# Places of an adding weight load, and of the sums and casts that wait for such loads, in a two-layer fp32 network kernel

## The chip, the cores and the metric

The kernel runs on one core of a Trainium2 chip. The metric is device time in microseconds of one execution; three executions of the kernel before gave 1048.98, 1050.86 and 1052.87, with a median of 1050.86.

The engines' names in the profile: PE multiplies matrices, DVE (VectorE) and ACT (ScalarE) work element by element, POOL (GpSimd) here issues mostly loads that add to what stands in the target, SP (SyncE) issues plain loads. Each engine works through its own list of instructions in order. A load is issued by an engine and then carried out by 16 DMA engines that all loads share.

## What is computed

The network has two residual layers over 512 tokens of 1024 features. Layer 0 mixes tokens by chunked attention, layer 1 by a gated linear recurrence. After each mixer comes the part that this case is about, a feed-forward block with a hidden size of 4096:

```python
D_MODEL = 1024; SEQ = 512; D_FF = 4 * D_MODEL

def rmsnorm(x, g):
    return x * lax.rsqrt(jnp.mean(x * x, axis=-1, keepdims=True) + RMS_EPS) * g

def sq_relu_mlp(h, w1, w2):
    z = jax.nn.relu(jnp.einsum('bsd,df->bsf', h, w1))
    return jnp.einsum('bsf,fd->bsd', z * z, w2)

for layer in range(2):
    h = h + mix[layer](rmsnorm(h, norm_mix[layer]))
    h = h + sq_relu_mlp(rmsnorm(h, norm_mlp[layer]), mlp_w1[layer], mlp_w2[layer])
return rmsnorm(h, norm_final)
```

All is float32.

## The kernel before

**Three matmuls for a product.** A float32 operand is split into a high part, rounded to the type that PE multiplies in one pass, and the rest, the low part. A product is made of high times high, high times low and low times high (`mm3`, L278 to L280). For weights, ACT makes the high part by a cast (`wh`, L178) and DVE the low part by a subtraction (`wl`, L181), piece by piece: a piece is 128 x 1024 numbers, 512 KB. There are five buffers each for `wh` and `wl`. The rows of the order below number the pieces: `wh47` and `wl47` are made from the 47th piece of the kernel.

**Fewer products by sums of blocks.** The feed-forward block multiplies 2 x 2 blocks in Strassen's manner, with seven products in place of eight, and some of the right operands are sums of weight blocks. For each group of the first weight matrix (`group(p, g)`, L806) the seven pieces are, in order: `u11`; `us1`, the sum of the blocks 21 and 22; `us2`, which is u11 + us1; `u12`; `us3`, which is u11 + 21; `us4`, u12 + us2; and `u22`. The second weight matrix gives seven pieces of two halves each: 11; t1, which is 12 + 11; 22; 21; t2; t3; t4. The plan (`add_mlp`, L237) mixes the two kinds in the order in which PE takes them.

Where the sums are made:
- `us1` needs no arithmetic engine: SP loads block 21 into the tile `kept` (L134), and POOL then issues a load of block 22 that adds to it (L136). The other half of `kept` takes block 22 alone.
- `us2` is a sum on DVE (L161). Behind it POOL issues the load of block 21 that adds to u11 in place, which makes `us3` (L163); it has to wait until `us2` and the `wl` of u11 have read u11.
- t1 is made by adding the loaded 11 to the loaded 12 by POOL's loads (`first_sum`, L123), t4 by one of L174. `us4`, t2 and t3 are sums on DVE.

**What sets the order.** The function `fetch` (L138) writes out, for the next piece, its sums, its cast and its subtraction, and then the loads that follow once its buffers are free. `want(1)` takes a piece and fetches on until three more are ready. The order in which an engine finally gets its instructions is made by the framework's scheduler from the order of the program and its own estimates; an instruction under `tc.keep_in_program_order` stays behind the instruction that the program writes just ahead of it on that engine.

**The first loads of a feed-forward block.** `first()` (L781) runs four pieces of the block's start (`up`), and there the attention or recurrence layer's residual tiles come free; one of them becomes `kept` for the groups from 1 on. Then come the loads of 11 and 12 of the second matrix (`load_down`, L118), the adding loads of `first_sum`, and group 0's second half (`group(0, 1)`) with, between its pieces, `opening`, the load of `kept` for group 1, the loads of 22 and 21, and `lengths`, eight sums of squares on ACT (`dsq`, L966) with the norm's reciprocal roots on DVE (`rq`, L776 to L779).

On PE, `m` are products of the first matrix (256 columns, 24 matmuls a piece), `x` and `y` of the second (512 columns). `a` is what the first matrix's products become by relu and square (L824, L825 on ACT, L820 a sum of two products on DVE). `hs`, `h` and `ls`, `l` are high and low parts of sums of `a`.

Of the kernel before, what the change touches and what calls it, by code (L numbers as in the profile page):

```python
# [35 lines left out]
def f(ap):  # L36
    return ap.bitcast(F32)
# [3 lines left out]
def trunk(ctx: ExitStack, tc: tile.TileContext, xT, cols, gfin, win, wqkv, wo, rwin, rga, rgx, rwo, w1, w2, out):  # L41
    nc = tc.nc
    V, S, G, PE = nc.vector, nc.scalar, nc.gpsimd, nc.tensor
# [57 lines left out]
    raws, start_, down, upper = {}, [], {}, {}  # L101

    def two(t):
        return t.rearrange("p (k c) -> p k c", k=2)

    def four(t):
        return t.rearrange("p (k c) -> p k c", k=4)

    def rows(src):
        return src.rearrange("(k p) c -> p k c", p=P)  # L110

    def load_down(key, name):
        if key not in down:
            return
        both = state["raw"].tile([P, 2, 1024], F32, name=f"b{name}_{key[0]}{key[1]}", tag=f"b{name}")
        for h in range(2):
            raws[name, h] = both[:, h]
            nc.sync.dma_start(two(raws[name, h]), rows(down[key][name][h * U : (h + 1) * U]))  # L118

    def first_sum(key):  # L120
        if key in down:
            for h in range(2):
                G.dma_start(raws["12", h], raws["11", h], accum_op=ALU.add)  # L123

    def load_up(key, name):
        if key not in upper:
            return
        if name in ("s1", "22"):
            raw = state["kept"][:, int(name == "22")]
        else:  # L130
            n = state["base"] + int(name == "12")
            raw = wraw.tile([P, 1024], F32, name=f"u{name}_{key[0]}{key[1]}", tag=f"wr{n % 3}")
        raws["u" + name] = raw
        nc.sync.dma_start(four(raw), rows(upper[key]["21" if name == "s1" else name]))  # L134
        if name == "s1":
            G.dma_start(four(raw), rows(upper[key]["22"]), accum_op=ALU.add)  # L136

    def fetch():  # L138
        i = state["next"]
        state["next"] += 1  # L140
        kind, nk, key = plan[i]
        H = wsp.tile([P, 1024], F32R, name=f"wh{i}", tag="wh")
        L = wsp.tile([P, 1024], F32R, name=f"wl{i}", tag="wl")
        n, half = 1024, nk
        if kind[:5] == "plain":
            n = nk * sum(src.shape[1] for src in key)
            raw = wraw.tile([P, 1024], F32, name=f"wr{i}", tag=f"wr{state['plain'] % 3}")
            state["plain"] += 1
            rv = raw[:, :n].rearrange("p (k c) -> p k c", k=nk)
            c0 = 0  # L150
            for n_, src in enumerate(key):
                w = src.shape[1]
                queue = nc.scalar if i == 0 and n_ else nc.sync
                queue.dma_start(rv[:, :, c0 : c0 + w], rows(src))
                c0 += w
        elif kind[0] == "u":
            nk = 4
            following = (key[0], key[1] + 1)
            if kind == "us2":
                raws["us2"] = wraw.tile([P, 1024], F32, name=f"us2_{key[0]}{key[1]}", tag=f"wr{(state['base'] + 2) % 3}")  # L160
                V.tensor_add(raws["us2"], raws["u11"], raws["us1"])  # L161
                raws["us3"] = raws["u11"]
                G.dma_start(four(raws["us3"]), rows(upper[key]["21"]), accum_op=ALU.add)  # L163
            if kind == "us4":
                raws["us4"] = raws["u12"]
                V.tensor_add(raws["us4"], raws["us4"], raws["us2"])
            raw = raws[kind]
        else:
            nk = 2
            following = (key[0], key[1] + 1)  # L170
            raw = raws[{"t1": "12", "t2": "22", "t3": "11", "t4": "21"}.get(kind, kind), half]
            if kind == "t2":
                V.tensor_add(raw, raw, raws["12", half])
                G.dma_start(raws["21", half], raw, accum_op=ALU.add)  # L174
            if kind == "t3":
                V.tensor_sub(raw, raws["22", half], raw)
        if i:
            S.copy(H[:, :n], raw[:, :n])  # L178
        else:
            start_.append(V.tensor_copy(H[:, :n], raw[:, :n]))  # L180
        low = V.tensor_sub(L[:, :n], raw[:, :n], f(H[:, :n]))  # L181
        if not i:
            start_.append(low)
        if kind == "plain_":
            state["base"] = state["plain"] % 3
            load_up((nk_layer[i], 0), "11")
            load_up((nk_layer[i], 0), "12")
        elif kind == "us2" and key[1]:
            load_up(following, "s1")
        elif kind == "us3":  # L190
            load_up(following, "11")
        elif kind == "us4":
            load_up(following, "12")
        elif kind == "u22" and key[1]:
            load_up(following, "22")
        elif kind == "t2" and half:
            load_down(following, "12")
        elif kind == "t3" and half:
            load_down(following, "11")
        elif kind == "t4" and half:  # L200
            first_sum(following)
            load_down(following, "22")
            load_down(following, "21")
        state["ready"].append((nk, H[:, :n].rearrange("p (k c) -> p k c", k=nk), L[:, :n].rearrange("p (k c) -> p k c", k=nk)))
# [466 lines left out]
    def mlp(ly, norm):  # L671
        with ExitStack() as mctx:
# [8 lines left out]
            low_, high = hB[0], hB[1]  # L681
# [68 lines left out]
            def up(p, j):  # L750
                WH, WL = want(1)
                acc = mmp(f"u{ly}{p}{j}")
                project([acc], [slice(0, P)], WH, WL, xs)
                for h in range(2):
                    if j % 4 == 0:
                        a[p, j // 4, h] = take(F32, f"a{p}{j // 4}{h}")
                    c = a[p, j // 4, h][:, j % 4]
                    S.activation(c, acc[:, h * U : (h + 1) * U], AF.Relu)
                    S.activation(c, c, AF.Square)
                if j == 0:  # L760
                    turn()
                if j == 1:
                    for k in range(KT):
                        scaled(k)
                if j == 2:
                    for n in (1, 3, 2, 4):
                        right(n)
                if j == 3:
                    for n in (1, 3, 2, 4):
                        right_split(n)  # L770
# [10 lines left out]
            def first():  # L781
                state["kept"] = sr.tile([P, 2, 1024], F32, name=f"kept0{ly}", tag="b21")
                load_up((ly, 0), "s1")
                load_up((ly, 0), "22")
                for j in range(4):
                    up(0, j)
                state["kept"] = per.tile([P, 2, 1024], F32, name=f"kept{ly}", tag="hx1")
                load_down((ly, 0), "11")
                load_down((ly, 0), "12")
                first_sum((ly, 0))  # L790
                here = group(0, 1)
                next(here)
                opening(0)
                load_up((ly, 1), "s1")
                next(here)
                load_down((ly, 0), "22")
                for n in range(4):
                    next(here)
                load_down((ly, 0), "21")
                load_up((ly, 1), "22")  # L800
                next(here)
                sums(0, False)
                sums(0, True)
                lengths()
# [56 lines left out]
            low, raw, turn_ = {}, {}, [0]  # L861
# [10 lines left out]
            def opening(p):  # L872
                raw["11"], raw["s1"], raw["s3"] = a[p, 0, 0], a[p, 0, 1], take(F32, f"s3{p}")
                ins = V.tensor_sub(raw["s3"], raw["11"], raw["s1"])
                if (ly, p) == (0, 1):
                    constants(ins)
                split("11", p)

            def sums(p, last):
                if last:  # L880
                    raw["s4"] = take(F32, f"s4{p}")
                    V.scalar_tensor_tensor(raw["s4"], raw["12"], -1.0, raw["s2"], ALU.mult, ALU.subtract)
                else:
                    raw["12"], raw["22"], raw["s2"] = a[p, 1, 0], a[p, 1, 1], take(F32, f"s2{p}")
                    V.tensor_sub(raw["s1"], raw["22"], raw["s1"])
                    V.scalar_tensor_tensor(raw["s2"], raw["22"], -1.0, raw["s3"], ALU.mult, ALU.subtract)
                    split("s1", p)
# [385 lines left out]
```

## Time and profile before

| | us |
|---|---|
| median of three executions | 1050.86 |
| the profiled execution | 1050.44 |
| its span, first to last instruction | 1048.7 |
| PE busy | 1023.1 |
| DVE busy | 876.6 |
| ACT busy | 667.2 |
| POOL busy | 91.0 |

The granted clock of PE was 0.992 of full speed on average. A row of a timeline has start, duration, engine, line of the kernel, operation, written and read tiles (without their numbers), and in brackets how long the engine had idled before and what released it. An engine may stand for long without loss where the work that it does later is not yet wanted; PE is the engine whose idle time counts as long as it is the busiest.

The times of loads are from issue to landing. With 0.5 MB each, a plain load of `kept` or `u` took 5.1 us in the median, an adding load of `kept` 6.0 and of `u` 6.3.

### The profile page before, as it was taken

Reading aid. Unit: us, or ns where it says so; the run is one execution under the profiler, and the core shown is the slowest. Engines: PE = TensorE matmul, PEld = TensorE weight load, DVE = VectorE, ACT = ScalarE, POOL = GpSimd, SP = SyncE. Lnnn points to the kernel's source line nnn. Section 1 sums busy time; section 2 is a strip of 40 time slices with the busy share of each in tenths; the row PEclk is TensorE's granted clock in tenths of the full one; section 3 lists DMA queues with packets and bytes.
Section 4 is the critical chain, followed back from the end, with each engine's and each line's share of the span. In section 5 each row is a group of like instructions: output and inputs, shape, how many; then the busy total and the mean of one; then the engine's idle time right before and its main releaser. Section 6 shows DMA issues by size and latency. Waiting matters only on the chain.

```text
span 1048.7 us, 15295 instructions
## 1 busy us (share of the span) xinstructions
PE 1023.1 (98%) x5762; PEld 894.3 (85%) x5762; DVE 876.6 (84%) x1230; ACT 667.2 (64%) x1020; POOL 91.0 (9%) x120
## 2 busy tenths in 40 slices
PE   9999999999899999999999999999899999999996
PEld 7788888888889999999987788888889999999985
DVE  7898779869489889789699989988389789789697
ACT  7667557647476567567567686656477567567565
POOL 1000000003101111111000000003101101101000
PEclk9999999999989999999999999999999999999999
DMA  8444354255948748737614412185848738737413
GB/s 270 114 129 132 82 165 116 61 148 134 240 101 219 177 87 220 202 61 202 181 21 114 128 61 81 58 231 124 230 101 221 201 61 221 202 61 201 122 41 100
DMA packets 122730, 147.34 MB, mean 140 GB/s; under 512 B 6304, under 2 KB 94368, under 8 KB 122656
## 3 DMA queue, kind: packets, MB, share of 16 engines
q1 hardware_dynamic: 101664, 112.09, 34.4%
q0 software_dynamic: 20416, 33.56, 18.5%
q8 instruction: 45, 0.74, 0.3%
q10 hardware_dynamic: 576, 0.72, 0.2%
q14 instruction: 29, 0.24, 0.1%
HBM read 119.07 MB, written 2.10 MB: 116 GB/s over the span
## 4 chain that ended last, share of the span: by engine, by line
PE 81%; DVE 9%; DMA 5%; issue 2%; SPq 1%; ACT 1%; POOL 0%; DVEq 0%; ACTq 0%; POOLq 0%
PE m L278 8%; PE m L280 8%; PE m L279 8%; PE x L279 5%; PE x L280 5%; PE x L278 5%; PE y L278 4%; PE y L279 3%; PE y L280 3%; DMA kept<-in_w 3%; DVE wl L181 3%; PE x L504 2%; PE wo L278 1%; PE wo L279 1%; PE v L278 1%
## 5 line engine op out<-in xcount | busy, mean ns | idle before, releaser
L178 ACT CAST wh<-b 128x1024 fp32r<-128x1024 f32 x112 | 117.0, 1052 | 85.6 <-PE m L279 44.2
L181 DVE TENSOR_TENSOR wl<-b,wh 128x1024 fp32r<-128x1024 f32 x112 | 136.1, 1222 | 39.2 <-ACT wh L178 38.5
L278 PE MATMUL m<-rH,wh 128*128 128x256 f32 x448 | 127.4, 284 | 12.7 <-DVE a L820 12.7
L280 PE MATMUL m<-rH,wl 128*128 128x256 f32 x448 | 127.1, 284 | 0.0
L279 PE MATMUL m<-rL,wh 128*128 128x256 f32 x448 | 127.0, 284 | 0.0
L278 PEld LDWEIGHTS m<-rH,wh 128*128 128x128 f32 x448 | 86.3, 193 | 14.3 <-DVE a L820 13.1
L178 ACT CAST wh<-wr 128x1024 fp32r<-128x1024 f32 (+1 forms) x65 | 66.7, 1029 | 44.6 <-PE wo L279 11.7
L280 PE MATMUL m<-hnH,wl 128*128 128x256 f32 x336 | 95.0, 283 | 0.0
L279 PE MATMUL m<-hnL,wh 128*128 128x256 f32 x336 | 95.0, 283 | 0.0
L278 PE MATMUL m<-hnH,wh 128*128 128x256 f32 x336 | 94.9, 282 | 0.0
L279 PEld LDWEIGHTS m<-rL,wh 128*128 128x128 f32 x448 | 86.4, 193 | 1.2
L280 PEld LDWEIGHTS m<-rH,wl 128*128 128x128 f32 x448 | 86.3, 193 | 0.0
L181 DVE TENSOR_TENSOR wl<-wr,wh 128x1024 fp32r<-128x1024 f32 (+1 forms) x66 | 78.1, 1187 | 7.7 <-ACT wh L178 7.4
L178 ACT CAST wh<-u 128x1024 fp32r<-128x1024 f32 x56 | 58.8, 1050 | 39.0 <-PE x L280 13.5
L181 DVE TENSOR_TENSOR wl<-u,wh 128x1024 fp32r<-128x1024 f32 x56 | 68.3, 1220 | 9.6 <-ACT wh L178 9.6
L279 PEld LDWEIGHTS m<-hnL,wh 128*128 128x128 f32 x336 | 64.3, 191 | 0.8
L278 PEld LDWEIGHTS m<-hnH,wh 128*128 128x128 f32 x336 | 64.2, 191 | 0.8
L280 PEld LDWEIGHTS m<-hnH,wl 128*128 128x128 f32 x336 | 64.3, 191 | 0.0
L278 PE MATMUL x<-wh,h 128*128 128x512 f32 (+1 forms) x132 | 50.8, 385 | 1.7 <-DVE d L1047 1.7
L279 PE MATMUL x<-wl,h 128*128 128x512 f32 (+1 forms) x132 | 50.9, 386 | 0.0
L280 PE MATMUL x<-wh,l 128*128 128x512 f32 (+1 forms) x132 | 50.9, 385 | 0.0
L278 PE MATMUL y<-wh,hs 128*128 128x512 f32 x128 | 50.2, 392 | 0.0
(382 smaller groups left out, 2894.9 us busy)
## 6 DMA issues: line engine op xcount, KB each, us to landing
b<-in_w SPq DMA_DIRECT2D x64, 512.0 KB, 5.9
b<-b POOLq DMA_DIRECT2D x32, 512.0 KB, 7.6
kept<-in_w SPq DMA_DIRECT2D x28, 512.0 KB, 5.1
u<-in_w SPq DMA_DIRECT2D x28, 512.0 KB, 5.1
wr<-in_wqkv SPq DMA_DIRECT2D x20, 512.0 KB, 4.1
wr<-in_rwin SPq DMA_DIRECT2D x16, 512.0 KB, 3.6
kept<-in_w POOLq DMA_DIRECT2D x14, 512.0 KB, 6.0
u<-in_w POOLq DMA_DIRECT2D x14, 512.0 KB, 6.3
```

The lines of the kernel that those rows point to most:

```text
L178: S.copy(H[:, :n], raw[:, :n])
L181: low = V.tensor_sub(L[:, :n], raw[:, :n], f(H[:, :n]))
L278: PE.matmul(acc, WH, XH, start=start, stop=False, skip_group_check=more)
L279: PE.matmul(acc, WH, XL, start=False, stop=False, skip_group_check=more)
L280: PE.matmul(acc, WL, XH, start=False, stop=stop, skip_group_check=more)
L504: PE.transpose(b[:, c : c + P], pt[:, seg[t] + kt * P : seg[t] + (kt + 1) * P], ident)
```

## The change

Three edits.

1. The sum `us2` on DVE stays behind what the program writes ahead of it on DVE.
2. So does the cast on ACT for the four kinds that have an adding load behind them: us1, us3, t1 and t4.
3. In `first()`, the plain load and the adding load of `kept` for group 1 are written ahead of the loads of 11 and 12, where they stood behind `opening`.

```diff
@@ fetch
             if kind == "us2":
                 raws["us2"] = wraw.tile([P, 1024], F32, name=f"us2_{key[0]}{key[1]}", tag=f"wr{(state['base'] + 2) % 3}")
-                V.tensor_add(raws["us2"], raws["u11"], raws["us1"])
+                tc.keep_in_program_order(V.tensor_add(raws["us2"], raws["u11"], raws["us1"]))
                 raws["us3"] = raws["u11"]
                 G.dma_start(four(raws["us3"]), rows(upper[key]["21"]), accum_op=ALU.add)
...
         if i:
-            S.copy(H[:, :n], raw[:, :n])
+            high = S.copy(H[:, :n], raw[:, :n])
+            if kind in ("us1", "us3", "t1", "t4"):
+                tc.keep_in_program_order(high)
@@ first
                 state["kept"] = per.tile([P, 2, 1024], F32, name=f"kept{ly}", tag="hx1")
+                load_up((ly, 1), "s1")
                 load_down((ly, 0), "11")
                 load_down((ly, 0), "12")
                 first_sum((ly, 0))
                 here = group(0, 1)
                 next(here)
                 opening(0)
-                load_up((ly, 1), "s1")
                 next(here)
```

Behind the second edit all lines stand two further down: L820 of before is L822 of the changed kernel.

What the edits move was read off the instructions of both programs, engine by engine. The rows have the line, the operation, and written and read tiles with their piece or block and a buffer number. First SP's queue in layer 0's feed-forward block, from the first load of block 12 of the second matrix. Before:

```order
L118 DMA b12_00_2765<-in_w2 128x2x512 x2
L134 DMA kept0_2761<-in_w1 128x4x256
L118 DMA b22_00_2843<-in_w2 128x2x512
L134 DMA u11_01_2816<-in_w1 128x4x256
L118 DMA b22_00_2843<-in_w2 128x2x512
L134 DMA kept0_2761<-in_w1 128x4x256
L134 DMA u12_01_2851<-in_w1 128x4x256
```

The same place of the changed program:

```order
L118 DMA b12_00_2767<-in_w2 128x2x512
L134 DMA kept0_2761<-in_w1 128x4x256
L118 DMA b12_00_2767<-in_w2 128x2x512
L118 DMA b22_00_2843<-in_w2 128x2x512 x2
L134 DMA kept0_2761<-in_w1 128x4x256
L134 DMA u11_01_2816<-in_w1 128x4x256
L134 DMA u12_01_2851<-in_w1 128x4x256
```

The first `kept` load (block 21 of group 1) has gone ahead of one half of b12, and u11 of group 1 now stands behind both halves of b22 and behind the second `kept` load (block 22). On POOL the adding load of `kept` has likewise gone between the two of b12. In layer 1 both halves of b22 stood ahead of u11 before as well, and only the second `kept` load has passed it.

DVE at the end of group 0, before:

```order
L181 TENSOR_TENSOR wl43_2847<-u12_00_2504,wh43_2846 128x1024
L161 TENSOR_TENSOR us2_01_3107<-u11_01_2816,kept0_2761 128x1024
L181 TENSOR_TENSOR wl44_2879<-kept00_2553,wh44_2878 128x1024
L181 TENSOR_TENSOR wl45_2910<-b11_00_2762,wh45_2909 128x1024
L181 TENSOR_TENSOR wl46_2940<-b11_00_2762,wh46_2939 128x1024
L820 TENSOR_TENSOR a011_0_2937<-m6001_2772,v001_2774 128x512
L181 TENSOR_TENSOR wl47_2975<-u11_01_2816,wh47_2974 128x1024
L820 TENSOR_TENSOR a011_0_2937<-m5001_2771,u001_2773 128x512
L181 TENSOR_TENSOR wl48_3040<-kept0_2761,wh48_3039 128x1024
```

In the changed program wl44 follows wl43 directly, and some rows behind wl47 stands:

```order
L888 SCALAR_TENSOR_TENSOR s20_0_3006<-a011_0_2937,s30_0_2806 128x1024
L870 TENSOR_TENSOR ls10_0_3010<-a001_0_2585,hs100_3009 128x1024
L778 TENSOR_TENSOR rq_97<-fs_99 128x4
L884 SCALAR_TENSOR_TENSOR s40_0_3013<-a010_0_2906,s20_0_3006 128x1024
L779 TENSOR_SCALAR rq_97<-rq_97 128x4
L183 TENSOR_TENSOR wl48_3040<-kept0_2761,wh48_3039 128x1024
L780 RECIPROCAL rq_97<-rq_97 128x4
L183 TENSOR_TENSOR wl49_3044<-b12_00_2767,wh49_3043 128x1024
L781 TENSOR_SCALAR nrq_98<-rq_97 128x4
L183 TENSOR_TENSOR wl50_3077<-b12_00_2767,wh50_3076 128x1024
L161 TENSOR_TENSOR us2_01_3107<-u11_01_2816,kept0_2761 128x1024
```

`us2` of group 1 has moved from ahead of wl44 to behind wl50, and wl48 from ahead of the sums of `a` and `s` to behind `s40`. In layer 1 the same rows have moved in the same way. In the groups of the later rounds `us2` stands two rows ahead of its own `wl`; before it stood further ahead.

ACT from the cast of u11 of group 1 on, before:

```order
L178 CAST wh47_2974<-u11_01_2816 128x1024
L824 ACTIVATE a011_0_2937<-a011_0_2937 128x512
L966 ACTIVATE dsq000_3015,fs_99<-d0_2550 128x512
L825 ACTIVATE a011_0_2937<-a011_0_2937 128x512
L966 ACTIVATE dsq001_3017,fs_99<-d0_2550 128x512
L178 CAST wh48_3039<-kept0_2761 128x1024
L824 ACTIVATE a011_0_2937<-a011_0_2937 128x512
L966 ACTIVATE dsq010_3019,fs_99<-d0_2550 128x512
```

Eleven rows later, behind the last of the eight squares, came the casts wh49 and wh50 of the two halves of t1 (b12). In the changed program the end of that stretch is:

```order
L968 ACTIVATE dsq021_3025,fs_99<-d0_2550 128x512
L827 ACTIVATE a010_0_2906<-a010_0_2906 128x512
L869 CAST hs100_3009<-a001_0_2585 128x1024
L968 ACTIVATE dsq030_3027,fs_99<-d0_2550 128x512
L968 ACTIVATE dsq031_3029,fs_99<-d0_2550 128x512
L178 CAST wh48_3039<-kept0_2761 128x1024
L178 CAST wh49_3043<-b12_00_2767 128x1024
L178 CAST wh50_3076<-b12_00_2767 128x1024
```

The cast of us1 (wh48) has moved behind all the squares; wh47, ahead of them, and wh49 stand where they stood. On PE the product of wh47 is followed by three `y` matmuls of wh49 in both programs, then by the product of wh48. No instruction is added or left out by the change.

## The prediction

> **What bounds the kernel now.** I read the page's busy table first, then the table of waits, then the two places that it points to on DVE and PE, then the granted clock there, then the queue that feeds them.
>
> ```profile
> span 1048.7 us, 15295 instructions
> PE 1023.1 (98%) x5762; PEld 894.3 (85%) x5762; DVE 876.6 (84%) x1230; ACT 667.2 (64%) x1020; POOL 91.0 (9%) x120
> DVE us L161 <- DMA kept<-in_w: 25.4, 2, 13.0
> PE m L278 <- DVE a L820: 12.7, 2, 6.7
> ```
>
> PE is busy for 98% of the span, so the time goes down only where PE idles or runs slowly. Its one large wait is the last row: 12.7 us, in two pieces. DVE's `us2` sum (L161) also waits twice, 25.4 us, for `kept`. The next rows show that the second wait causes the first. First the MLP of layer 0, on DVE:
>
> ```profile
> 285.57 1.23 DVE L161 TENSOR_TENSOR us<-u,kept 128x1024 f32<-128x1024 f32 x1 [13.01 <-DMA kept<-in_w]
> ...
> 290.12 0.68 DVE L820 TENSOR_TENSOR a<-m,v 128x512 f32<-128x512 f32 x1
> 290.72 1.22 DVE L181 TENSOR_TENSOR wl<-u,wh 128x1024 fp32r<-128x1024 f32 x1
> ...
> 302.15 1.23 DVE L181 TENSOR_TENSOR wl<-b,wh 128x1024 fp32r<-128x1024 f32 x1
> ```
>
> and PE at that time, then both at the same place of layer 1:
>
> ```profile
> 283.93 0.28 PE L280 MATMUL m<-hnH,wl 128*128 128x256 f32 x1
> 290.86 0.58 PE L278 MATMUL m<-rH,wh 128*128 128x256 f32 x1 [6.65 <-DVE a L820]
> ...
> 295.29 0.39 PE L278 MATMUL x<-wh,h 128*128 128x512 f32 x1
> 295.51 0.40 PE L279 MATMUL x<-wl,h 128*128 128x512 f32 x1
> ```
>
> ```profile
> 757.05 1.22 DVE L161 TENSOR_TENSOR us<-u,kept 128x1024 f32<-128x1024 f32 x1 [12.40 <-DMA kept<-in_w]
> 756.03 0.28 PE L280 MATMUL m<-hnH,wl 128*128 128x256 f32 x1
> 762.34 0.58 PE L278 MATMUL m<-rH,wh 128*128 128x256 f32 x1 [6.03 <-DVE a L820]
> 766.55 0.40 PE L278 MATMUL x<-wh,h 128*128 128x512 f32 x1
> ```
>
> DVE works in order. While it sits 13.01 us in front of `us2`, wl44 to wl46 and the sum `a011` (L820) stand behind it, although nothing that they read is late; `us2` itself is first used as wl51, two pieces of PE work after wl49. PE runs out at 284.05 (283.93 + 0.12, the start-to-start distance of 256-column matmuls at full clock) and gets on at 290.86: 6.81 us. The piece that then runs has 24 such matmuls, 2.88 us at full clock, but takes 295.29 - 290.86 = 4.43. The windows of 3.4 us say why:
>
> ```profile
> 290.70:294.20 3.50, 3.34 (x15) 3.34 (x16) 1.85 (x4) 3.36 (x8) 1.29 (x1) 0.51 0.50 186
> 755.00:758.40 3.40, 1.31 (x11) 1.10 (x10) 1.35 (x2) 0.23 (x1) 0.00 (x0) 0.99 0.67 225
> 758.40:761.80 3.40, 0.00 (x0) 0.00 (x0) 3.40 (x4) 0.00 (x0) 0.00 (x0) 0.50 0.31 85
> ```
>
> The third number from the end is the granted clock. While the first piece after the stall runs it is at half, which costs 1.55 us here. So the site loses 6.81 + 1.55 = **8.4 us**; in layer 1 it is 762.34 - 756.15 = 6.19 and 4.21 - 2.88 = 1.33, **7.5 us**. Together **15.9 us** can be won, about 1.5%. (Some 0.5%, 5 us, is what a measurement of this kernel can tell from no change.)
>
> **What the change removes.** In the program of the changed kernel `us2` stands behind wl50 on DVE, in both layers, and all that stood behind it at 285.57 runs as its weights are cast, before PE asks for it. Both stalls go, with their clock: **-15.9 us**.
>
> **What it adds at the same two places.** SP's queue is the one to read, since moving the `kept` load also moves what follows it. The two parts are of layer 0 and of layer 1; the rows of landing after them are the answers for the short stretch in which each was issued.
>
> ```profile
> 269.15 0.37 SPq L134 DMA_DIRECT2D u<-in_w  x1
> 269.56 0.51 SPq L118 DMA_DIRECT2D b<-in_w  x1
> 270.11 0.50 SPq L134 DMA_DIRECT2D kept<-in_w  x1
> ...
> 737.24 0.88 SPq L118 DMA_DIRECT2D b<-in_w  x2
> 741.25 0.37 SPq L134 DMA_DIRECT2D u<-in_w  x1
> 741.66 0.88 SPq L134 DMA_DIRECT2D kept<-in_w  x1
> ```
>
> ```profile
> u<-in_w SPq DMA_DIRECT2D x1, 512.0 KB, 9.4
> b<-in_w SPq DMA_DIRECT2D x1, 512.0 KB, 12.8
> kept<-in_w SPq DMA_DIRECT2D x1, 512.0 KB, 15.3
> u<-in_w SPq DMA_DIRECT2D x1, 512.0 KB, 12.8
> kept<-in_w SPq DMA_DIRECT2D x1, 512.0 KB, 16.1
> ```
>
> In layer 0, u11 of group 1 was issued at 269.15 (when its buffer came free) and landed 9.4 later, at 278.6; the second half of b22 landed at 282.4, the second `kept` load ("22") at 285.4: in the order of issue. The changed program puts b22's second half and that `kept` load **ahead** of u11. u11's buffer is freed no sooner, so u11 takes the last slot of the three, 285.4 at the latest. In layer 1 only the `kept` load is passed: u11 goes from 754.1 to at most 757.8. The loads now ahead can start some 2 us sooner, but the DMA engines had little room:
>
> ```profile
> 260.00:268.00 8.00, 8.00 (x41) 6.79 (x41) 6.38 (x7) 4.39 (x9) 0.59 (x1) 1.00 1.03 237
> 276.00:284.00 8.00, 8.00 (x69) 8.00 (x67) 0.00 (x0) 4.25 (x6) 0.00 (x0) 1.00 1.12 252
> ```
>
> Share 1.03 against 1.12: at most 9% of 8 us and of the next 8 is free, 1.4 us. I take half: u11 lands at L = **284.7** and **757.1**.
>
> Who waits for u11? The cast wh47 on ACT, wl47 on DVE, and all behind them. On ACT that is the work below, which before began at 290.84 and now begins when wh47 is done, L + 1.05:
>
> ```profile
> 281.25 1.05 ACT L178 CAST wh<-u 128x1024 fp32r<-128x1024 f32 x1 [0.68 <-PE m L279]
> 290.84 0.63 ACT L824 ACTIVATE a<-a 128x512 f32<-128x512 f32 x1 [8.54 <-DVE a L820]
> ...
> 300.74 1.99 ACT L178 CAST wh<-b 128x1024 fp32r<-128x1024 f32 x2
> ```
>
> From 290.84 to wh49 at 300.74 it is 9.9 us, the same instructions in both programs (wh48 is only moved to the end of them). On DVE the time from wl47's start to wl49's end was 302.15 + 1.22 - 290.72 = 12.65 us. wl47 now starts at L + 1.05, and wl48, which ran in a gap before, must come between (its cast is pinned behind the squares): 1.14, less 0.3 of slack that was there. So wl49 is ready at **L + 14.5**. PE, without the old stall, wants it for the second `y` matmul: 284.05 + 2.88 (wh44) + 5.5 (24 `x` matmuls of 512 columns at 0.23) + 2.88 (wh47) + 0.23 = **295.5**; in layer 1, 756.15 + 11.49 = **767.6**. The new stalls are 284.7 + 14.5 - 295.5 = **3.7** and 757.1 + 14.5 - 767.6 = **4.0 us**. Bounds: wh47's buffer is free at 281.25, so not under 0.3; with u11 in the very last slot 4.4 and 4.7.
>
> The clock after a new stall: in layer 1 the window 755.0 to 758.4 still had 1.31 us of PE work and 0.99, and the next one was at 0.50. So about 2 us of idleness in one window was enough, and stalls of 3.7 and 4.0 can trip it. Ends: nothing, and two windows of 3.4 us at half, 3.4 us. I take what the two old stalls paid, 1.4 each (they are the nearest rows): **+2.8 us**. The Trainium skill (TensorE: Matmul & The Clock Gate, "Why this matters for your kernels") sets the bound for such drops at gaps of over about 3 us, one idle window; by that rule both stalls would also trip it if they come as worked out, and neither if u11 lands 1 us sooner, where the sum would be 2.8 us better. The row at 755.0 shows a drop after a shorter idle stretch than the rule's, so I keep the term.
>
> **The rest, at nothing.** In later rounds `us2` moves to two rows ahead of its own `wl`, and the `us3` transfer (L163) follows it. The rows of one such round:
>
> ```profile
> 382.29 1.22 DVE L181 TENSOR_TENSOR wl<-us,wh 128x1024 fp32r<-128x1024 f32 x1
> 390.61 0.28 PE L280 MATMUL m<-rH,wl 128*128 128x256 f32 x1
> DMA to landing us min/median/max: 5.6/6.3/8.0
> 391.31 1.05 ACT L178 CAST wh<-u 128x1024 fp32r<-128x1024 f32 x1
> ```
>
> The sum puts 1.14 us ahead of wl79 (the first row), which then ends at 384.6 against a first use at 390.61: hidden under 6 us. The adding transfer, free to go once the sum is done at about 382.3, takes 5.6 to 8.0 us by the third row, so it lands at 388 to 390.3, ahead of its cast at 391.31: hidden by 1 to 3 us at each of 12 places. The pinned casts otherwise keep places they had. The instructions are the same in number.
>
> **Sum.** -15.9 + 3.7 + 4.0 + 2.8 = -5.4. From the profiled execution's 1050.44 (its span 1048.7, 1.7 around it; the median of the runs is 1050.86, 0.4 more) that is **1045.0 us**.
>
> **The rivals.**
>
> 1. *No new wait.* u11 lands early enough (by about 281.3 and 754), because the adding transfers of POOL's queue finish sooner or SP's queue doesn't keep its order. Against it: every landing above is in order, and 260 to 284 is full. Then only the lower bounds remain: -15.9 + 0.3 + 1.0, and no clock: **1036 us**.
> 2. *The wait only changes its name*, or the pinned sum doesn't do what it says. u11 in the last slot (4.4 + 4.7) and two half-clock windows at each site (6.8) eat 15.9 whole: **1050.4 us**. For it: the idle stretch before the drop at 758.4.
> 3. *Slower: the adding transfers of the rounds.* At 12 places the transfer now waits for the later sum. If it is as slow as the one beside the first loads,
>
> ```profile
> 272.28 13.27 DMA kept<-in_w
> ```
>
> it lands at 395.6, 4.3 us behind 391.31, and the cast, now pinned, holds ACT's later rows with it. It decides from a transfer of 9 us on. If 1 us of each shows on PE, 12 us: 1045 + 12 = **1057 us**. Against it: the slowest in the row of the rounds is 8.0.
>
> **How the numbers follow.** The forecast, new stalls of 3 to 5 us with or without the clock, has a chance of 0.62, over 1041 to 1049; it is cut by the 0.5% mark (1045.6) almost in the middle. Rival 1 has 0.18, rival 2 0.12, rival 3 0.08. Faster by over 0.5%: 0.36 of the forecast and rival 1, 0.54. Within 0.5%: the other 0.26 and rival 2, 0.38. Slower: 0.08. The range, 1035.5 to 1050.4, goes from rival 1 to the upper bounds of the unknown terms and leaves rival 3 out.
>
> **What would show it.** DVE's wait at L161 for `kept` is gone from the table of waits, and PE's for `a` (L822 there) too. In their place ACT's wh47 (`wh<-u`) or DVE's wl47 waits for `u<-in_w` until about 284.7 and 757.1, and PE waits 3 to 5 us for a `wl<-b` before a `y` matmul near 295.5 and 767 less what was won, with the clock near 0.5 behind it. u11's landing time is the first thing to look at: under 282, rival 1. If `wh<-u` casts wait for POOL's L163 transfers at many places, rival 3. I am wrong altogether if PE still stops at `a`, or if a stall stands where the trace of before has none.

## The result and the profile after

The changed kernel took **1043.72 us** in the median of four executions (1042.31 to 1044.33), against 1050.30 of four executions before (1048.98 to 1052.87). The ratio is 0.9932, with a 95% interval of 0.991 to 0.9955: 6.6 us or 0.7% faster. The forecast was 1045.0.

The page of the changed kernel, its first and its third line, and the waits of PE that are over 1.7 us in the table of waits (for what, us in total, times, the longest):

```profile
span 1041.8 us, 15285 instructions
PE 1024.3 (98%) x5762; PEld 894.6 (86%) x5762; DVE 875.2 (84%) x1230; ACT 665.4 (64%) x1020; POOL 91.2 (9%) x120
```

```profile
PE y L280 <- ACT wh L178: 2.7, 1, 2.7
...
PE x L280 <- DVE d L747: 2.0, 2, 1.3
...
PE x L280 <- DVE d L1049: 1.8, 1, 1.8
```

PE's 12.7 us for the sum `a` are gone, and so is the row of DVE's wait for `kept` at L161. A wait of the `y` matmuls for a cast stands in their place, once and not twice, and a new small one for `d`, twice. (The last row was there before.) The place in layer 0, on PE, then on ACT and DVE:

```profile
283.88 0.28 PE L282 MATMUL m<-hnH,wl 128*128 128x256 f32 x1
284.00 0.28 PE L280 MATMUL m<-rH,wh 128*128 128x256 f32 x1
...
298.01 0.49 PE L280 MATMUL y<-wh,hs 128*128 128x512 f32 x1 [2.67 <-ACT wh L178]
299.87 0.80 PE L281 MATMUL y<-wl,hs 128*128 128x512 f32 x1 [1.36 <-DVE wl L183]
```

```profile
285.94 1.05 ACT L178 CAST wh<-u 128x1024 fp32r<-128x1024 f32 x1 [5.41 <-DMA u<-in_w]
...
287.02 1.22 DVE L183 TENSOR_TENSOR wl<-u,wh 128x1024 fp32r<-128x1024 f32 x1 [5.01 <-ACT wh L178]
...
298.62 1.19 DVE L183 TENSOR_TENSOR wl<-b,wh 128x1024 fp32r<-128x1024 f32 x1
```

The old stall of 6.81 us is wholly gone: PE goes on at 284.00 without a pause. The forecast chain is there instead. wh47 waits for the load of u11 until 285.94, wl49 (the row at 298.62) ends at 299.81, which is 13.9 us behind wh47's start (forecast: 14.5 behind the landing), and PE loses 298.01 - 295.18 = 2.83 us and 299.87 - 298.01 - 0.23 = 1.63 us at the first two `y` matmuls (295.18 is where a run of matmuls without a gap gets to): 4.45 us, where 3.7 was forecast and 4.4 was the bound. (PE's own order isn't wholly that of before: between the products of wh47 and wh48 stand four `y` matmuls in the changed kernel and three in the kernel before, and it differs at the ends of the blocks too.) The half clock is there as well, in parts of these two windows:

```profile
297.40:300.80 3.40, 1.43 (x3) 1.02 (x4) 3.40 (x7) 3.40 (x5) 0.00 (x0) 0.84 0.01 2
300.80:304.20 3.40, 3.40 (x20) 3.21 (x19) 3.40 (x4) 2.49 (x4) 1.29 (x1) 0.65 0.20 46
```

By the start of the same `y` matmul in both traces (307.44 before, 305.00 after) layer 0's place won 2.4 us net: the old loss of 8.4 is gone, and a new one of 6.0 has come, 4.45 of it idle and the rest, 1.6, at half clock. In layer 1 the cast that should have waited is this one, and the row of wl49 follows (layer 0's names are kept for the same pieces of layer 1):

```profile
752.29 1.05 ACT L178 CAST wh<-u 128x1024 fp32r<-128x1024 f32 x1 [1.18 <-DMA u<-in_w]
...
764.98 1.19 DVE L183 TENSOR_TENSOR wl<-b,wh 128x1024 fp32r<-128x1024 f32 x1
```

wh47 has its weights at 752.2, not at 757.1. From there the chain is as long as in layer 0: wl49 ends at 766.17, 13.9 us behind wh47's start. PE gets to the first `y` matmul at 765.77 and waits 0.2 us at the second, so **PE does not stall in layer 1**. The first `x` matmul there starts at 757.42 against 766.55: the lead over the kernel before is 9.1 us, and just ahead of the old stall it was 1.6 (754.46 against 756.03). So layer 1 gave 7.6 us, where 2.1 was forecast. At the end of the span only 6.9 us are left of the 9.1, and between the two layers 0.9 of the 2.4 went as well. These points, layer 1 and the losses behind the two places, are what the experiments had to explain, beside who puts u11 where it is.

### The profile page after: what moved, and what is told of

It is laid out like the page before. It is cut to its first block, busy times and chain, and to the rows that moved or that the text cites. A ratio compares the mean times of both kernels' runs of the same rounds, so it can differ in the third digit from the quotient of the medians.

```text
span 1041.8 us, 15285 instructions
## 1 busy us (share of the span) xinstructions
PE 1024.3 (98%) x5762; PEld 894.6 (86%) x5762; DVE 875.2 (84%) x1230; ACT 665.4 (64%) x1020; POOL 91.2 (9%) x120
## 4 chain that ended last, share of the span: by engine, by line
PE 86%; DVE 5%; DMA 3%; ACT 3%; issue 2%; ACTq 0%; DVEq 0%; SPq 0%
PE m L282 8%; PE m L281 8%; PE m L280 8%; PE x L280 5%; PE x L281 5%; PE x L282 5%; PE y L281 4%; PE y L282 4%; PE y L280 4%; DMA u<-in_w 2%; DVE wl L183 2%; PE x L506 2%; PE wo L280 1%; PE wo L281 1%; PE ro L282 1%
## 5 line engine op out<-in xcount | busy, mean ns | idle before, releaser
L281 PE MATMUL y<-wl,hs 128*128 128x512 f32 x128 | 50.5, 394 | 1.4 <-DVE wl L183 1.4
```

The lines of the kernel that those rows point to most:

```text
L281: PE.matmul(acc, WH, XL, start=False, stop=False, skip_group_check=more)
```

## The experiments

The change has three edits, and the second holds two pairs of kinds. The runs take them apart. Ratios are to the kernel before, run again beside them (its median was 1051.82 us beside the four rows from the sum alone on and 1051.26 beside the last four), with their 95% intervals.

| kernel | sum us2 | casts us1, us3 | casts t1, t4 | load of kept | us, median | ratio |
|---|---|---|---|---|---|---|
| changed | pinned | pinned | pinned | moved | 1043.72 | 0.9932 (0.991 to 0.9955) |
| sum alone | pinned | - | - | - | 1036.70 | 0.9864 (0.9845 to 0.9883) |
| casts alone | - | pinned | pinned | - | 1058.25 | 1.0055 (1.0037 to 1.0073) |
| load alone | - | - | - | moved | 1043.84 | 0.9922 (0.9907 to 0.9936) |
| first sums free | from group 1 on | pinned | pinned | moved | 1048.15 | 0.9965 (0.9952 to 0.9978) |
| sum and load | pinned | - | - | moved | 1034.42 | 0.9842 (0.9827 to 0.9857) |
| u casts only | pinned | pinned | - | moved | 1040.94 | 0.9901 (0.9886 to 0.9915) |
| t casts only | pinned | - | pinned | moved | 1037.52 | 0.9873 (0.9858 to 0.9888) |
| u11 first | pinned | pinned | pinned | moved | 1036.63 | 0.9858 (0.9841 to 0.9874) |

### The sum alone

The changed kernel without its second and third edit:

```diff
-            if kind in ("us1", "us3", "t1", "t4"):
-                tc.keep_in_program_order(high)
...
-                load_up((ly, 1), "s1")
                 load_down((ly, 0), "11")
...
                 opening(0)
+                load_up((ly, 1), "s1")
```

> Only the sum us2 is kept in program order; the casts are free and the load of kept stays where it was. Theory A (the pinned casts put u11 behind the second kept load and wh48 behind the squares; the sum alone removes the two old stalls): both waits of us2 for kept and of PE for the sum a are gone, u11 of group 1 lands near 279 and in layer 1 well before PE wants it, no stall before the y matmuls, so 1050.3 - 15.9 = 1034.5 us, up to 1037 if the ends of the two blocks keep what they lost in the changed kernel. Theory B (the moved load puts u11 behind, or the moved load is what makes the gain): either no difference to the changed kernel (1043.7) or us2 waits for kept behind wl50 and PE with it (1042 to 1048).

1036.7 us. Theory A holds: both old stalls are gone, no `y` matmul waits, and the ends of the blocks lose nothing. One edit of one line gives 14 of the 15.9 us that the prediction put on the table. u11 landed at 282.1, not near 279. What is missing is one new pause, at the row

```profile
274.22 0.39 PE L278 MATMUL m<-rH,wh 128*128 128x256 f32 x1 [1.84 <-ACT m L838]
```

where PE waits for a copy on ACT (L838). That copy stands on ACT behind wh42, and ACT waited for wh42's weights until 269.58: POOL's adding load to u11 of group 0 landed at 269.50.

### The casts alone

```diff
-                tc.keep_in_program_order(V.tensor_add(raws["us2"], raws["u11"], raws["us1"]))
+                V.tensor_add(raws["us2"], raws["u11"], raws["us1"])
...
-                load_up((ly, 1), "s1")
                 load_down((ly, 0), "11")
...
                 opening(0)
+                load_up((ly, 1), "s1")
```

> Only the four kinds of casts are kept in program order. Theory A: u11 lands behind the second kept load (near 285 in layer 0), us2 stands between wl44 and wl45 and still waits for kept until 285.5, so wl45 comes about 1 us late for the x matmuls, and behind it wl49 comes 3 to 5 us late for the y matmuls, with half clock for some of it: a gain of 2 to 3 us in each layer, 1045 to 1047 us. Theory B (casts are harmless): the old stalls as in the kernel before, about 1050.

**Slower than before**, by 0.55%, and a miss for both theories. DVE and PE in layer 0, and PE in layer 1:

```profile
285.03 1.22 DVE L161 TENSOR_TENSOR us<-u,kept 128x1024 f32<-128x1024 f32 x1 [10.22 <-DMA kept<-in_w]
286.18 2.35 DVE L183 TENSOR_TENSOR wl<-b,wh 128x1024 fp32r<-128x1024 f32 x2
```

```profile
289.19 0.58 PE L280 MATMUL m<-rH,wh 128*128 128x256 f32 x1 [5.14 <-DVE a L822]
...
763.84 0.58 PE L280 MATMUL m<-rH,wh 128*128 128x256 f32 x1 [5.47 <-DVE a L822]
```

I had counted on wl44 standing ahead of `us2`, which it does here, and on PE so having its next piece. But the piece of wh44 also waits for the sum `a` (L822), since it adds on to the accumulator that this sum reads, and that sum stands behind `us2`, wl45 and wl46 as ever. So the old stalls stay nearly whole, 5.1 and 5.5 us of 6.7 and 6.0. To that come the losses of the pinned casts in the rounds and at the ends of the blocks. u11 landed at 284.7, behind the second `kept` load (281.3): **the pinned casts alone reorder SP's queue**, without the moved load.

The traces show what comes between a cast and that queue. These are wh42, the cast of us3, and wl42, in the kernel before; then both and the load of u11 in this one:

```profile
266.81 1.05 ACT L178 CAST wh<-u 128x1024 fp32r<-128x1024 f32 x1 [3.19 <-PE u L279]
...
267.90 1.22 DVE L181 TENSOR_TENSOR wl<-u,wh 128x1024 fp32r<-128x1024 f32 x1 [1.48 <-ACT wh L178]
```

```profile
268.97 1.05 ACT L178 CAST wh<-u 128x1024 fp32r<-128x1024 f32 x1
...
270.45 2.35 DVE L183 TENSOR_TENSOR wl<-u,wh 128x1024 fp32r<-128x1024 f32 x2
...
271.70 1.50 SPq L134 DMA_DIRECT2D u<-in_w  x2
```

wh42's weights had landed at 265.7 and 265.4. The pinned wh42 runs behind work on ACT that it ran ahead of before (relu and square of `a`, and the cast of `h`), and wl42, the first of the two in its row, behind two other rows of DVE. wl42 is the last to read the buffer that u11 of group 1 takes: in the five kernels where its row stands alone, the load of u11 is issued 0.02 to 0.04 us behind its end. So u11 can be loaded from 271.70, not from 269.15, and the loads of b22 and of `kept`, which do not need this buffer, stand ahead of it. That the scheduler chose their order for this reason is likely but not shown. (With the sum alone the buffer came free as late, at 271.92, since wh42 had to wait for POOL's load: there u11 kept its place in the queue and landed at 282.1.)

### The load alone

```diff
-                tc.keep_in_program_order(V.tensor_add(raws["us2"], raws["u11"], raws["us1"]))
+                V.tensor_add(raws["us2"], raws["u11"], raws["us1"])
...
-            if kind in ("us1", "us3", "t1", "t4"):
-                tc.keep_in_program_order(high)
```

> Only the load of kept is moved ahead. us2 still stands ahead of wl44. Theory A: the adding load of kept is second instead of third on POOL and lands 3 to 4 us sooner (near 282 in layer 0), so each old stall shrinks from 6.8 and 6.2 to about 3 us; with the clock the gain is 3 to 4.5 us for each layer, 1042 to 1044 us; u11 lands ahead of the second kept load as before. Theory B: u11 goes behind, with a wait of its own, and the gain is under 4 us in all, 1046 to 1050.

1043.84 us, as theory A had it. u11 landed at 278.6, ahead of the second `kept` load, as in the kernel before; the adding load of `kept` landed at 282.2 where it was 285.6, and in layer 1 at 748.4 where it was 757.0. The old stalls shrink, and layer 1's more than forecast, to 0.9 us at the old place and 1.3 at a `y` matmul:

```profile
287.48 0.58 PE L278 MATMUL m<-rH,wh 128*128 128x256 f32 x1 [3.62 <-DVE a L820]
...
754.55 0.39 PE L278 MATMUL m<-rH,wh 128*128 128x256 f32 x1 [0.88 <-DVE a L820]
...
767.50 0.50 PE L279 MATMUL y<-wl,hs 128*128 128x512 f32 x1 [1.27 <-DVE wl L181]
```

So moving the load is worth some 8 us by itself, and the 1.3 us at the `y` matmul are the only new wait of PE. It and the pinned sum are two cures for one stall: together they can't give the sum of both.

### The first sums free

The changed kernel, with `us2` of group 0 of each layer free:

```diff
-                tc.keep_in_program_order(V.tensor_add(raws["us2"], raws["u11"], raws["us1"]))
+                twice = V.tensor_add(raws["us2"], raws["u11"], raws["us1"])
+                if key[1]:
+                    tc.keep_in_program_order(twice)
```

> The changed kernel, but the sum us2 of each block's first group (group 0) isn't kept in program order; POOL's load that adds to u11 then stands ahead of the 16 loads of the turned residual in layer 1 again, as in the kernel before. Theory C (the loads of layer 1 started some 6 us sooner because that adding load no longer stood ahead of the turned residual's on POOL): they start late again, u11 lands near 755 to 757 by the old clock of the span, and PE stalls 3 to 4 us ahead of the y matmuls of layer 1, with 1 to 1.5 us for the clock: 1043.7 + 5 = 1048 to 1049. Rival D (they started sooner for another reason, such as the moved load or the pinned casts): 1043.7, unchanged.

1048.15 us: theory C. Why layer 1's loads were late or early is seen in the queues of SP and POOL at the block's start. First the kernel before, then the changed one, then this one, each with the loads of the turned residual (`d<-turned`, 16 on each queue), POOL's adding load to u11 (`u<-in_w`) and SP's first load of b12:

```profile
721.25 13.85 SPq L738 DMA_DIRECT2D d<-turned  x16
735.42 0.89 SPq L118 DMA_DIRECT2D b<-in_w  x2
...
720.68 1.30 POOL L163 DMA_DIRECT2D u<-in_w  x1 [27.20 <-DVE wl L181]
721.84 3.92 POOL L738 DMA_DIRECT2D d<-turned  x7
```

```profile
717.05 10.48 SPq L740 DMA_DIRECT2D d<-turned  x16
727.85 0.37 SPq L118 DMA_DIRECT2D b<-in_w  x1
...
717.68 8.62 POOL L740 DMA_DIRECT2D d<-turned  x16 [26.25 <-ACT rH L703]
726.91 1.36 POOL L163 DMA_DIRECT2D u<-in_w  x1 [0.61 <-issue]
```

```profile
719.50 14.48 SPq L742 DMA_DIRECT2D d<-turned  x16
...
718.92 1.30 POOL L165 DMA_DIRECT2D u<-in_w  x1 [28.11 <-DVE wl L185]
720.09 3.92 POOL L742 DMA_DIRECT2D d<-turned  x7
```

In the kernel before, the adding load of 512 KB stands ahead of the small loads. They begin at 721.25 and take SP 13.85 us; in the changed kernel they begin at 717.05 and take 10.48. So b12, with POOL's adding loads that wait for it, starts 735.42 - 727.85 = 7.6 us sooner, 6.0 of it beyond the lead that PE had by then. 4.2 us is the sooner start: DVE makes the last turned blocks ahead of, not behind, `us2` and the `wl` of u11, at 716.6 where it was 720.8. 3.4 us is the shorter run without the 512 KB beside it: in the four kernels of this document with that sum free the 16 loads took SP 13.3 to 14.5 us, in the six with it pinned 10.3 to 10.6. The load of u11 itself is not issued sooner (741.25 before, 742.40 in the changed kernel, 742.20 in this one); it landed when the loads beside it had landed. In the changed kernel the last of POOL's adding loads there had landed at 750.7 and u11 landed at 752.2; in this one they landed at 755.8 and 755.6. With group 0's sum free both come back (a start at 719.50, with PE 1.8 us ahead of the kernel before, and 14.48 us), and with them the stall:

```profile
767.79 0.50 PE L282 MATMUL y<-wh,hs 128*128 128x512 f32 x1 [2.06 <-ACT wh L180]
769.64 0.80 PE L283 MATMUL y<-wl,hs 128*128 128x512 f32 x1 [1.35 <-DVE wl L185]
```

Which of the two parts would be enough was not tried.

### The sum and the load, no casts

```diff
             high = S.copy(H[:, :n], raw[:, :n])
-            if kind in ("us1", "us3", "t1", "t4"):
-                tc.keep_in_program_order(high)
```

> The sum us2 pinned and the load of kept moved, no cast pinned. u11 of group 1 stands ahead of the second half of b22 and of the second kept load, the squares stand behind wh48 again. Theory A (only the pinned casts cost anything): no stall ahead of the y matmuls in either layer, nothing lost at the ends of the two blocks, 6 + 2 us under the changed kernel: 1035 to 1036 us. With the sum alone PE stood 2.0 us at 274 for wh42, since POOL's load that adds to u11 landed at 269.5 beside both halves of b12; here one half of b12 stands behind kept, so that stall should be gone or under 1 us. Rival: the moved load costs as much elsewhere as it saves there, 1036.7 as with the sum alone or more.

**1034.42 us**, the best of all, 1.6% under the kernel before. No `y` matmul waits and PE doesn't stop at `a`. The pause at 274 is down from 1.84 to 0.47 us of idle (PE waits there for the copy on ACT behind wh42, not for a product of wh42 itself):

```profile
272.69 0.39 PE L278 MATMUL m<-rH,wh 128*128 128x256 f32 x1 [0.47 <-ACT m L838]
```

POOL's adding load to u11 landed at 268.0, not at 269.5.

### The casts of the first matrix only, and of the second only

```diff
-            if kind in ("us1", "us3", "t1", "t4"):
+            if kind in ("us1", "us3"):
```

> The changed kernel with only the casts of us1 and us3 pinned, those of t1 and t4 free. Theory A: the pinned casts of the first matrix are what puts u11 behind the second kept load and wh48 behind the squares, so the stall of 4.4 us with its clock ahead of the y matmuls of layer 0 stays; the ends of the two blocks, where only t1 and t4 have pinned casts, lose nothing: 1043.7 - 1.5 to 2 = about 1042 us. Rival: the ends lose because DVE is full there whatever is pinned, 1043.7.

```diff
-            if kind in ("us1", "us3", "t1", "t4"):
+            if kind in ("t1", "t4"):
```

> The changed kernel with only the casts of t1 and t4 pinned, those of us1 and us3 free. Theory A: u11 lands before 282 in layer 0 and nothing stalls ahead of the y matmuls: 6 us less, 1037.7; the ends of the two blocks lose 1.5 to 2 us as in the changed kernel, with PE waiting there for DVE's d (L747). Rival: the ends lose nothing with these alone, about 1036.

1040.94 and 1037.52 us: the two losses part cleanly. Against 1034.42 without pinned casts, those of us1 and us3 cost 6.5 us and those of t1 and t4 3.1; all four cost 9.3. With us1 and us3 pinned PE waits for wh49 and wl49 in layer 0 as in the changed kernel, and nothing at the ends. With t1 and t4 pinned there is no such wait, and PE waits for `d` at both ends of the blocks. These are the rows of the changed kernel, then of the one with t1 and t4 alone:

```profile
563.26 0.47 PE L280 MATMUL x<-wh,h 128*128 128x512 f32 x1 [1.28 <-DVE d L747]
...
1021.18 0.47 PE L280 MATMUL x<-wh,hs 128*128 128x512 f32 x1 [0.77 <-DVE d L747]
```

```profile
558.03 0.47 PE L280 MATMUL x<-wh,h 128*128 128x512 f32 x1 [1.30 <-DVE d L747]
...
1015.64 0.47 PE L280 MATMUL x<-wh,hs 128*128 128x512 f32 x1 [0.76 <-DVE d L747]
```

Neither row is in the profiles of the sum alone, of the load alone, of the sum and the load, or of the casts of us1 and us3. `d` is written by DVE, whose order at the end of the block differs with the pins. In the changed kernel DVE works there without a wait, and the `d` that PE waits for stands behind two rows of `wl`:

```profile
560.09 1.22 DVE L183 TENSOR_TENSOR wl<-b,wh 128x1024 fp32r<-128x1024 f32 x1
561.23 1.22 DVE L183 TENSOR_TENSOR wl<-wr,wh 128x1024 fp32r<-128x1024 f32 x1
562.36 1.41 DVE L747 SCALAR_TENSOR_TENSOR d<-x,nrq,d 128x512 f32<-128x512 f32 x2
```

It starts at 562.36, hardly sooner than its counterpart in the kernel before (562.53), though PE is 2.5 us ahead. PE's own order at the ends of the blocks differs as well, in the kernels with the casts of t1 and t4 pinned and in no other. Which of the two orders makes the wait was not separated.

### u11 first

The changed kernel with all its pins, and SP's loads of b22 and of the second half of `kept` pinned behind that of u11:

```diff
-            nc.sync.dma_start(two(raws[name, h]), rows(down[key][name][h * U : (h + 1) * U]))
+            load = nc.sync.dma_start(two(raws[name, h]), rows(down[key][name][h * U : (h + 1) * U]))
+            if name == "22" and not key[1]:
+                tc.keep_in_program_order(load)
...
-        nc.sync.dma_start(four(raw), rows(upper[key]["21" if name == "s1" else name]))
+        load = nc.sync.dma_start(four(raw), rows(upper[key]["21" if name == "s1" else name]))
+        if name == "22" and key[1] == 1:
+            tc.keep_in_program_order(load)
```

> The changed kernel with all its pins, and the loads of b22 and the second load of kept pinned behind u11's load on SP. Theory E (the new stall of layer 0 comes from u11's place in SP's queue alone): u11 lands near 278, wh47 begins when its buffer is free at 281.3, wl49 is ready at about 295.3, PE's stall ahead of the y matmuls is under 0.5 us and the clock stays: 6 us less than the changed kernel, 1037.7 us. Rival F (the place of wh48 behind the squares makes the stall): a stall of 1 to 4 us stays, 1039 to 1043. The loads of b22 and kept start some 6 us later; their casts come 20 us after, so they should not be missed.

1036.63 us, 7 us under the changed kernel with every pin in place. wh47 and the `y` matmul that stalled:

```profile
282.01 1.05 ACT L182 CAST wh<-u 128x1024 fp32r<-128x1024 f32 x1 [2.12 <-DMA u<-in_w]
```

```profile
295.95 0.51 PE L285 MATMUL y<-wl,hs 128*128 128x512 f32 x1 [1.00 <-DVE wl L187]
```

u11 landed at 281.9, later than the 278 expected but 3.9 us sooner than in the changed kernel, and the stall shrank by as much or nearly, from 4.45 us to 1.0 of idle, with the clock at full. wh48 stood behind the squares here too. So theory E holds for all but that 1 us. By the first row u11 still came 2.1 us behind the point where ACT was free for it. Its load is first in the queue here, but was issued at 271.18, 2.0 us later than in the kernel before: with wh42 pinned, wl42 freed the buffer as late as described under the casts alone. The 2.2 us by which the kernel with the sum and the load alone is faster still are about the two waits for `d` at the ends of the blocks, which this kernel has too (2.0 us).

## Why the prediction came out right, and where it was wrong

**The old stalls: right.** Both went with their half clock. The sum alone, which does nothing else, gave 14.

**The new stall in layer 0: right in its mechanism, a little under in its size.** u11 landed at 285.84, and the sum as worked out (+ 14.5 - 295.5) gives a stall of 4.8 for that; 4.45 was measured, as against 3.7 forecast. The chain behind the landing took 14.0 us, not 14.5. u11 took the last slot (the bound was 285.4), and the half-share of room that I gave it, 0.7 us, was not there. "u11's buffer is freed no sooner" hid a change: it was freed 2.7 us later (271.81 against 269.15). The clock cost 1.6 us where 1.4 was forecast.

**Its cause: wrong.** The prediction said that "moving the `kept` load also moves what follows it". The load alone leaves u11 where it was, with or without the pinned sum; the pinned casts of us1 and us3 move it, probably through the buffer that wl42 frees later. Pinned casts do so without the other two edits as well as with them. I read the order of the two programs, which differ in three edits at once, and named the one that deals with loads. The price was right because the order was read and not derived; the advice that would have followed (don't move the load) would have been wrong.

**The new stall in layer 1: the step that failed.** "In layer 1 only the `kept` load is passed: u11 goes from 754.1 to at most 757.8" took the landing times of layer 1's loads from the trace of before. u11 landed at 752.2. b12, ahead of it, began 7.6 us sooner, since the pinned sum of group 0 went behind the turned residual's blocks on DVE and its adding load behind their loads on POOL; with that sum free u11 lands at 755.6 and the stall is back. The wait for u11 and the length of the chain behind it were right in layer 1 too: what failed was the landing, off by 4.9 us. I had the order of POOL's queue at that place before me and gave it no price. This term was 4.0 + 1.4 us and measured 0.2.

**The rest "at nothing": wrong by about 3 us.** "The pinned casts otherwise keep places they had" held for the casts, not for what the scheduler did around them. Those of t1 and t4 let PE wait for `d` at both ends of the blocks. Between the two places the lead falls by 0.9 us, and in layer 1 from 9.1 to 7.7 in the last `x` products (1034.77 against 1027.04) and to 6.9 at the end of the span, the last 0.8 of it by a clock drop (below). In sum: layer 0 won 2.4 where 3.3 was forecast, layer 1 7.6 where 2.1 was, and the rest lost 3.1 where nothing was. The errors largely cancel, and that is luck: the forecast of 1045.0 for 1043.72 is better than its parts.

**The rivals.** No wait (rival 1) is what layer 1 did, and what the kernel would have done in both without the casts. The wait that only changes its name (rival 2) is nearly what layer 0 did: of 8.4 us only 2.4 were won. Late adding transfers in the rounds (rival 3) did not come: in the changed kernel's table of waits ACT's `wh` casts wait for `u<-in_w` twice, 6.6 us in all, and these are the two waits of wh47 shown above (5.41 and 1.18). With the casts alone the rounds lost a little, at waits for `d`.

## What to carry to other kernels

Where several edits go in together, price each one's effect on every queue by itself: here one of them won 14 us, a second won 8 by curing the same stall in another way, and the third took back 9. Keeping an instruction that waits for a late load in its place in the program frees those behind it; keeping one in place that could run sooner delays the buffer that it frees, and the price appears elsewhere, on a load queue or at the end of a block. And a stall that has been cured in one place moves the start of everything that follows, so a second place can't be priced from the old trace's times alone: work out there too what the queue's first entry waits for, and when the buffer of the load in question comes free.

## What the runs showed of the hardware

In all ten kernels SP's weight loads (L118 and L134 of the kernel before) landed in the order in which SP issued them.

Nearly the same pause, ahead of the last `x` matmuls, cost different amounts in different kernels. The windows of before and of the changed kernel around it:

```profile
1039.80:1043.20 3.40, 1.69 (x12) 1.49 (x12) 2.51 (x7) 2.03 (x6) 0.00 (x0) 1.00 0.24 93
```

```profile
1032.80:1036.20 3.40, 2.65 (x12) 2.36 (x12) 1.97 (x7) 2.03 (x6) 0.00 (x0) 0.62 0.29 113
```

Pauses of 1.82 and 1.95 us precede the same matmuls; the clock stayed full in the first and fell to half in the second, where the 12 matmuls of the window took 2.65 us in place of 1.69. With the casts alone a pause of 1.96 us at that place was followed by half clock too; pauses of 1.93 (the first sums free), 1.96 (t casts only) and 1.97 us (u11 first) left it full. So the length of the pause alone doesn't decide: at about 2 us of idleness it went either way here. In layer 0 stalls of 2.83 and 1.63 us, one directly behind the other, brought 3.4 us of half clock in the changed kernel (299.7 to 303.2), and nearly the same pair (2.59 and 1.63) with the u casts only brought 6.8 (298.1 to 305.0).
